# A hybrid attention and mixture-of-experts layer on one core: the weight units' place in memory, and the place of a conditional part

## The chip, the core and the metric

The kernel runs on one core of a Trainium2 chip. The time is the device time of one execution in microseconds (us), the median of several runs. One core has a matrix engine (TensorE, PE in the profile; PEld is its weight load), a vector engine (VectorE, DVE), a scalar engine (ScalarE, ACT), GpSimd (POOL), and SyncE (SP), which here only issues transfers. 16 DMA engines move data between the chip's main memory (HBM) and the core's on-chip memory (SBUF: 128 partitions). TensorE writes to PSUM, eight banks of 128 x 512 float32.

## The reference

One layer over 256 latent tokens of 1024 features, with 256 context tokens. The front half is a modulated layer norm, one input projection, neighbourhood attention beside a spatial gating unit, an output projection and a layer norm. The back half, where the change is, is a mixture of 32 experts with four chosen for each token:

```python
def moe_ffn(h, router_w, router_b, w_gu, b_gu, w_down, b_down):
    logits = t @ router_w + router_b
    top_vals, top_idx = lax.top_k(logits, TOP_K)          # 4 of 32
    gates = jax.nn.softmax(top_vals, axis=-1)
    ...
    def expert_step(acc, xs):
        gu = t @ wgu + bgu                                # 1024 x 2048
        gate = jnp.minimum(gu[:, :D_FF_EXPERT], SWIGLU_LIMIT)
        lin = jnp.clip(gu[:, D_FF_EXPERT:], -SWIGLU_LIMIT, SWIGLU_LIMIT)
        y = ((lin + 1) * (gate * jax.nn.sigmoid(SWIGLU_ALPHA * gate))) @ wd + bd   # 1024 x 1024
        return acc + wgt[:, None] * y, None
...
x = layer_norm(DEEPNORM_ALPHA * x + g2 * ffn_x, ln2_g, ln2_b)
```

All is float32. An expert's weights are 12 MB, those of all experts 384 MB (in units of 2^20 bytes), and each is read once.

## The kernel before

**Groups and slots.** Experts are ranked on the chip by how many tokens chose them, and worked off in 13 groups: group 0 holds experts 0 and 1, then come groups of one, two or four ranks in the order of `PLAN` (L35). A group always makes one matmul of 128 token slots: one rank has 128 slots, each of a pair 64, each of four 32. The last group, number 12, has four ranks. For every group the tokens are gathered by a one-hot matmul (`gather`), go through four gate-up steps (`gu_step`, L1105, each over 512 columns, with `swiglu_gate` or `swiglu_lin` behind it), are transposed (`h_T`), go through the down projection in two halves of 512 columns (`down`, L1152), are scaled by the gate vector (`scaled`, L1184) and are added to the accumulator `acc` by a one-hot matmul (`scatter`, L1165). The scatter of a group is put off into the next one (`pending`, run at its hook "gu1"). The last group does its own: it scatters the first half between the two halves of `down`, and its second half is added in two PSUM banks, `sums`, that an identity matmul of `acc` has started (`last_sums`, L1178, at the hook "in2", in the middle of the group's gate-up part).

**The conditional part.** Tokens beyond a rank's slots are taken by `overflow_items` (L1238): every engine loads the number of items, and under `tc.If(n_items > 0)` (L1240) a loop runs one more group of 128 slots for each item, weights and all. With the inputs of this case the number is zero and the body is skipped. The part stands ahead of group 5 (the second group of one rank). Ahead of it, group 4's scatter is run at once, and from group 4 on four weight units are kept free for the loop's own loads (`reserve[0] = 4`, L1318).

**Weights.** SBUF holds 26 units (`NU`, L38) of 128 x 2048 float32, 8 KB in each partition, in the pool `uni`. A unit is taken for a weight piece or for other data. Pieces stand in one list, `stream`, in the order of use; `pump` (L138) takes a free unit and has SyncE issue the load, and `done` (L151) releases a unit behind its last matmul and pumps the next piece. One expert is eight gate-up pieces and four down pieces of 1 MB; in the last group the second half's later pieces are cut smaller (`DOWN_ROWS`, L37). SyncE works its list in order: an issue waits until the unit's last reader is done. In the last group, six units hold other data.

**Order.** The order of instructions on each engine is that of the program text (`manual_schedule`). The pools are placed in SBUF in the order of their making: the constants, `cst`, come first, then `uni`. Constants are rounded up to 32 bytes.

Of the kernel before, what the change touches and what calls it, by code (L numbers as in the profile page):

```python
# [9 lines left out]
F32 = mybir.dt.float32  # L10
# [8 lines left out]
P = 128  # L19
# [3 lines left out]
TT = NTOK // P  # L23
# [14 lines left out]
NU = 26  # L38
# [27 lines left out]
def hybrid_layer_kernel(  # L66
# [12 lines left out]
    router_w = router_w[0]  # L79
    w_gu, b_gu, w_dn, b_dn = exp_w_gu, exp_b_gu[0], exp_w_down, exp_b_down[0]  # L80

    cst = ctx.enter_context(tc.tile_pool(name="cst", bufs=1))
    uni = ctx.enter_context(tc.tile_pool(name="uni", bufs=1))
    mo = ctx.enter_context(tc.tile_pool(name="mo", bufs=2))
    sm = ctx.enter_context(tc.tile_pool(name="sm", bufs=4))
    pm = ctx.enter_context(tc.tile_pool(name="pm", bufs=4, space=bass.MemoryType.PSUM))
# [5 lines left out]
    def nm(s):  # L92
        uid[0] += 1
        return f"{s}_{uid[0]}"

    def mm_bank():
        return pm.tile([P, 512], F32, tag="mm", name=nm("mm"))
# [40 lines left out]
    def pump(n=1, keep=0):  # L138
        while n > 0 and stream and len(free_slots) > keep:
            key, fn = stream.pop(0)  # L140
            t = unit("w")
            loaded[key] = (t, fn(t))
            n -= 1
# [12 lines left out]
    reserve = [0]  # L156
# [2 lines left out]
        return bass.AP(tensor=src.tensor, offset=src.offset, ap=[[0, parts], [1, n]])  # L159


    ident = cst.tile([P, P], F32, name="ident")
    make_identity(nc, ident)
    mhalf = cst.tile([P, 1], F32, name="mhalf")
    G.memset(mhalf, -0.5)


# [551 lines left out]
    late, zst = {}, {}  # L719
# [445 lines left out]
    def scatter(ys, st, nns=range(2)):  # L1165
        for nn in nns:
            t2_free(ys[nn])
            for t in range(TT):
                b = ax_bank()
                PE.matmul(b, st[:, t, :], ys[nn], start=True, stop=True)  # L1170
                sl = acc[t][:, nn * 512:(nn + 1) * 512]
                V.tensor_tensor(sl, sl, b, op=ALU.add)  # L1172
                if zst2:
                    ln_half(zst2[t], acc[t], nn)
# [3 lines left out]
    def last_sums():  # L1178

        for t in range(TT):  # L1180
            sums.append(ax_bank())
            PE.matmul(sums[t], ident, acc[t][:, 512:D], start=True, stop=False)

    def scaled(bank, nn):  # L1184
        y = t2("y")
        t2_hold(y)
        V.tensor_tensor(y, bank, late_v["g2"][:, nn * 512:(nn + 1) * 512], op=ALU.mult)  # L1187
        return y

    def group(n, gid, cur, sel, hooks):  # L1190
        xg = cur[0]

        def hook(name):
            for f in hooks.get(name, ()):
                f()

        b = gu_step(n, gid, 0, 0, xg, sel, lambda: hook("in0"))
        if gid == 0:
            hook("gu0")
        g_0 = swiglu_gate(b)  # L1200
        if gid != 0:
            hook("gu0")
        b = gu_step(n, gid, 1, 0, xg, sel, lambda: hook("in1"))
        l_0 = swiglu_lin(b, g_0)
        hook("gu1")
        b = gu_step(n, gid, 0, 1, xg, sel, lambda: hook("in2"))
        g_1 = swiglu_gate(b)
        h0 = h_T(l_0)
        hook("gu2")
        b = gu_step(n, gid, 1, 1, xg, sel, lambda: hook("in3"))  # L1210
        l_1 = swiglu_lin(b, g_1)
        yb = [mm_bank() for _ in range(2)]
        if gid == len(groups) - 1:
            hs = (h0, h_T(l_1))
            zst2.extend(sm.tile([P, 2, 6], F32, tag="zst", bufs=2, name=nm("zst")) for _ in range(TT))
            down(n, gid, hs, 0, yb[0], last=True)
            ys = [scaled(yb[0], 0)]
            scatter(ys, cur[1], [0])
            down(n, gid, hs, 1, yb[1], last=True)
            y = scaled(yb[1], 1)  # L1220
            for t in range(TT):
                PE.matmul(sums[t], cur[1][:, t, :], y, start=False, stop=True)
                V.bn_stats(zst2[t][:, 1, :], sums[t])
            return None
        hs = [h0]
        down(n, gid, hs, 0, yb[0], 0, 4)
        hs.append(h_T(l_1))
        down(n, gid, hs, 0, yb[0], 4)
        ys = [scaled(yb[0], 0)]
        down(n, gid, hs, 1, yb[1])  # L1230
        for h in hs:
            t2_free(h)
        ys.append(scaled(yb[1], 1))
        return lambda: scatter(ys, cur[1])
# [3 lines left out]
    def overflow_items():  # L1238
        n_items = nc.values_load(nit[0:1, 0:1], min_val=0, max_val=NE)
        with tc.If(n_items > 0):  # L1240
            with tc.For_i(0, n_items) as it:
                ps_ = mo.tile([P, 2, TT, 1], F32, tag="ipos", bufs=1, name="ipos")
                for a in range(2):
                    V.tensor_copy(ps_[:, a], late_v["itm"][:, a, :, ds(it, 1)])
                sc_ = mo.tile([P, 1], F32, tag="isel", bufs=1, name="isel")
                V.tensor_copy(sc_, prs_[:, ds(it, 1)])
                ie = mo.tile([1, 1], I32, tag="iexp", bufs=1, name="iexp")
                V.tensor_copy(ie, iei[0:1, ds(it, 1)])
                rest = stream[:]
                stream.clear()  # L1250
                group_stream("x", [(ie, 0)])
                oh = make_oh(ps_[:, 0], 1, P)
                sel = make_sel(sc_)
                xg = gather(oh)
                st = weigh_T(weigh(oh, ps_[:, 1]))
                group(1, "x", (xg, st), sel, {})()
                stream.extend(rest)
# [5 lines left out]
    for gi, rk in enumerate(groups):  # L1263
        n = 2 if rk is None else len(rk)
        nxt = groups[gi + 1] if gi + 1 < len(groups) else None
        box = {}
        hooks = {k: [] for k in ("in0", "gu0", "in1", "gu1", "in2", "gu2", "in3")}

        def prep():
            a, m = nxt[0], len(nxt)  # L1270
            box["oh"] = make_oh(late_v["pcr"][:, 0, :, a:a + m], m, P // m)
            box["sel"] = make_sel(perm[:, a:a + m])
            box["ohg"] = weigh(box["oh"], late_v["pcr"][:, 1, :, a:a + m])

        def fetch():
            box["cur"] = [gather(box["oh"]), None]
            box["cur"][1] = weigh_T(box["ohg"])

        def streams():
            for g2_, rk2 in enumerate(groups[1:], 1):  # L1280
                group_stream(g2_, [(ordi, rr) for rr in rk2], g2_ == len(groups) - 1)
            pump(NU)

        def first_T():
            cur[1] = weigh_T(ohg0)

        if gi == 0:
            hooks["in0"] += [rank_counts]
            hooks["gu0"] += [rank_order, streams]
            hooks["gu1"] += [finish_G]  # L1290
            hooks["in1"] += [lambda: by_rank(late_v["pcr"], perm[0:NE, :])]
            hooks["gu1"] += [first_T, prep]
        else:
            if nxt:
                hooks["gu0"] += [prep]
            hooks["gu1"] += [pending]
        if gi == 1:
            hooks["in0"] += [lambda: acc_init((0, 1))]
            hooks["gu0"] += [lambda: acc_init((2, 3))]
            reserve[0] = 2  # L1300
        if gi == 2:
            ovf_u, l2_u = unit("ovf"), unit("l2")
            reserve[0] = 0
            for k, f in zip(("in0", "in1", "in2", "in3"), overflow_steps(ovf_u[:, 0:512])):
                hooks[k] += [f]
            S.dma_start(l2_u[0:1, 0:D], ln2_g)
            S.dma_start(l2_u[0:1, D:2 * D], ln2_b)
        if nxt:
            hooks["gu2"] += [fetch]
        if gi == 4:  # L1310
            def spread(js):
                for j in js:
                    b = ax_bank()
                    PE.matmul(b, ident[0:1, 0:1].to_broadcast([1, P]), l2_u[0:1, j * 512:(j + 1) * 512], start=True, stop=True)
                    S.copy(l2_u[:, j * 512:(j + 1) * 512], b)
            hooks["in1"] += [lambda: spread((0, 1))]
            hooks["in2"] += [lambda: spread((2, 3))]
            reserve[0] = 4  # L1318
        if gi == 5:
            pending()  # L1320
            hooks["gu1"].remove(pending)
            overflow_items()

            xg_i[0] ^= 1
            mo.tile([P, TT, P], F32, tag="sT", name=nm("sT"))
            mo.tile([P, 1, P], F32, tag="sel", name=nm("sel"))
            reserve[0] = 0
            pump(NU)
        if gi == len(groups) - 1:
            hooks["in2"] += [last_sums]  # L1330
        pending = group(n, gi, cur, sel_now, hooks)
        if gi == 2:
            release(ovf_u)
            pump(1)
        if nxt:
            cur, sel_now = box["cur"], box["sel"]
# [80 lines left out]
```

## Time and profile before

| what | us |
|---|---|
| median of 3 runs | 1139.0 (1137.99 to 1139.81) |
| the profiled execution, its own time | 1136.04 |
| its span, first to last instruction | 1134.3 |
| TensorE matmuls busy | 997.4 (88%) |
| VectorE busy | 306.0 (27%) |
| ScalarE busy | 132.8 (12%) |

The transfers are 451 MB (10^6 bytes), a mean of 398 GB/s over the span. In the profile a line such as L1160 is that of the source; a group of instructions is written as output <- inputs by the program's names, with the count and the busy time, and in brackets the idle time just before it and what ended it. `w` is a weight unit, `mm` and `ax` are PSUM banks, `t` a scratch tile. A float32 matmul appears as two matmul records. "PEclk" is the TensorE clock that was granted, as a share of the full one. A DMA share of 1.00 means that all 16 engines are busy, and it can come out slightly over that.

### The profile page before, as it was taken

Reading aid. Unit: us, or ns where it says so; the run is one execution under the profiler, and the core shown is the slowest. Engines: PE = TensorE matmul, PEld = TensorE weight load, DVE = VectorE, ACT = ScalarE, POOL = GpSimd, SP = SyncE. Lnnn points to the kernel's source line nnn. Section 1 sums busy time; section 2 is a strip of 40 time slices with the busy share of each in tenths; the row PEclk is TensorE's granted clock in tenths of the full one; section 3 lists DMA queues with packets and bytes.
Section 4 is the critical chain, followed back from the end, with each engine's and each line's share of the span. In section 5 each row is a group of like instructions: output and inputs, shape, how many; then the busy total and the mean of one; then the engine's idle time right before and its main releaser. Section 6 shows DMA issues by size and latency. Waiting matters only on the chain. (4 is left out here: it accounts for less than half of the span.)

```text
span 1134.3 us, 13253 instructions
## 1 busy us (share of the span) xinstructions
PE 997.4 (88%) x5140; PEld 421.6 (37%) x5140; DVE 306.0 (27%) x621; ACT 132.8 (12%) x286; POOL 27.7 (2%) x57
## 2 busy tenths in 40 slices
PE   5999897999779999986799999987799999977765
PEld 4897465333214433321253434222134343421111
DVE  6596765314103121210121212111021211201003
ACT  4343342100100101110010101000001010100000
POOL 2000300000000000000000000000000000000000
PEclk9999898999989999988999999988899999999988
DMA  9998599799999999999989999999999999999995
GB/s 381 421 396 325 229 360 366 307 386 422 420 421 421 421 420 421 422 420 421 420 343 422 421 421 420 421 422 421 421 422 420 420 422 420 421 422 421 421 420 190
DMA packets 66296, 451.32 MB, mean 398 GB/s; under 512 B 8627, under 2 KB 8883, under 8 KB 12725
## 3 DMA queue, kind: packets, MB, share of 16 engines
q1 hardware_dynamic: 66082, 450.03, 96.4%
q8 instruction: 42, 0.69, 0.2%
q10 hardware_dynamic: 148, 0.40, 0.1%
q14 instruction: 24, 0.20, 0.0%
HBM read 449.36 MB, written 1.05 MB: 397 GB/s over the span
## 5 line engine op out<-in xcount | busy, mean ns | idle before, releaser
L1114 PE MATMUL mm<-w,xg 128*32 128x512 f32 (+2 forms) x2048 | 424.9, 620 | 42.7 <-DMA w<-in_exp_w_gu_dram 42.7
L1160 PE MATMUL mm<-w,t 128*32 128x512 f32 (+2 forms) x1024 | 235.2, 645 | 52.2 <-DMA w<-in_exp_w_down_dram 43.6
L1114 PEld LDWEIGHTS mm<-w,xg 128*32 128x32 f32 (+2 forms) x2048 | 127.9, 130 | 325.6 <-issue 242.4
L1160 PEld LDWEIGHTS mm<-w,t 128*32 128x32 f32 (+2 forms) x1024 | 67.4, 133 | 207.9 <-issue 109.9
L1187 DVE TENSOR_TENSOR t<-mm,late 128x512 f32<-128x512 f32 x26 | 18.0, 692 | 263.0 <-PE mm L1160 263.0
L1130 ACT ACTIVATE t<-t 128x512 f32<-128x512 f32 x26 | 16.4, 630 | 583.0 <-DVE t L1128 583.0
L1137 DVE TENSOR_SCALAR t<-mm 128x512 f32<-128x512 f32 x26 | 18.0, 692 | 222.7 <-PE mm L1114 222.7
L1128 DVE TENSOR_SCALAR t<-mm 128x512 f32<-128x512 f32 x26 | 18.0, 691 | 215.4 <-PE mm L1114 215.4
L894 PE MATMUL mm<-bgu,sel 32*128 32x512 f32 x104 | 58.4, 641 | 4.0 <-PEq L1240 4.0
L1170 PE MATMUL ax<-t,sT 128*128 128x512 f32 x100 | 46.3, 605 | 0.8 <-DVE t L1187 0.8
L888 PE MATMUL ax<-oh,tM 128*128 128x128 f32 x384 | 44.8, 275 | 0.0
L888 PEld LDWEIGHTS ax<-oh,tM 128*128 128x128 f32 x384 | 43.8, 192 | 0.0
L1149 ACT COPY t<-ax 128x512 f32<-128x512 f32 x26 | 15.0, 576 | 190.6 <-PE ax L1145 190.6
L245 POOL TENSOR_TENSOR rs<-rs,mhalf 128x1 f32<-128x1 f32 x12 | 9.5, 797 | 1047.4 <-DVE mv L257 919.5
L1172 DVE TENSOR_TENSOR xin<-xin,ax 128x512 f32<-128x512 f32 x50 | 33.2, 684 | 5.2 <-PE ax L1170 4.8
L1170 PEld LDWEIGHTS ax<-t,sT 128*128 128x128 f32 x100 | 18.0, 189 | 29.2 <-issue 24.6
L894 PEld LDWEIGHTS mm<-bgu,sel 32*128 32x128 f32 x104 | 15.3, 183 | 34.3 <-issue 24.5
L780 ACT ACTIVATE xg<-ax,sh,sc 128x128 f32<-128x128 f32 x60 | 22.4, 457 | 32.3 <-PE ax L888 26.5
L414 DVE TENSOR_TENSOR wlo<-w,whi 128x1024 fp32r<-128x1024 f32 x20 | 23.7, 1223 | 3.1 <-ACT whi L411 3.1
L411 ACT CAST whi<-w 128x1024 fp32r<-128x1024 f32 x20 | 20.1, 1047 | 9.5 <-PE mm L446 9.5
L1145 PEld LDWEIGHTS ax<-ident,t 128*128 128x128 f32 x104 | 11.2, 141 | 21.8 <-issue 16.8
L525 DVE SCALAR_TENSOR_TENSOR accB<-w,front,accB 128x2048 f32<-128x2048 f32 x8 | 18.8, 2348 | 0.0
(261 smaller groups left out, 717.8 us busy)
## 6 DMA issues: line engine op xcount, KB each, us to landing
w<-in_exp_w_gu_dram SPq DMA_DIRECT2D x256, 1024.0 KB, 19.8
w<-in_exp_w_down_dram SPq DMA_DIRECT2D x124, 1024.0 KB, 19.8
w<-in_w_front_dram SPq DMA_DIRECT2D x38, 1024.0 KB, 10.7
w<-in_exp_w_down_dram SPq DMA_DIRECT2D x4, 512.0 KB, 16.1
w<-in_exp_w_down_dram SPq DMA_DIRECT2D x8, 256.0 KB, 6.9
T<-in_rpb_dram SPq DMA_DIRECT2D x2, 768.0 KB
xin<-in_x_dram SPq DMA_DIRECT2D x2, 512.0 KB
cin<-in_ctx_dram SPq DMA_DIRECT2D x2, 512.0 KB, 6.4
```

The source lines that it names most:

```text
L411: S.copy(av[:, k], w[:, k])
L414: V.tensor_tensor(bv[:, k], w[:, k], av[:, k].bitcast(F32), op=ALU.subtract)
L525: V.scalar_tensor_tensor(accB_u, w[:, 0, :], sT[:, k, 0:1], accB_u, op0=ALU.mult, op1=ALU.add)
L780: S.activation(dst[:, kk, :], src, AF.Identity, scale=sc2[:, kk:kk + 1], bias=sh2[:, kk:kk + 1])
L888: PE.matmul(bank[:, k * P:(k + 1) * P], late["tMv"][:, t, (hh * 4 + k) * P:(hh * 4 + k + 1) * P], oh[:, t].rearrange("p n w -> p (n w)"), ...
L894: PE.matmul(b, sel[r, :], bgu[r, :], start=True, stop=False)
L1114: PE.matmul(b[a * w:(a + 1) * w, :], xg[:, half * 4 + k, a * w:(a + 1) * w], weights((gid, part, j, half, a))[:, k, :], start=False, stop= ...
L1128: V.tensor_scalar_min(gtile, b, 7.0)
L1137: V.tensor_scalar(lt, b, 7.0, -7.0, op0=ALU.min, op1=ALU.max)
L1160: PE.matmul(bank[a * w:(a + 1) * w, :], hs[kk // 4][:, kk % 4 * P + a * w:kk % 4 * P + (a + 1) * w], weights((gid, nn, r0, a))[:, k, :], s ...
L1170: PE.matmul(b, st[:, t, :], ys[nn], start=True, stop=True)
L1172: V.tensor_tensor(sl, sl, b, op=ALU.add)
```

## The change

First, the pool `uni` is made ahead of `cst`, behind a new pool `pad` of 128 bytes that holds the small constant `mhalf`; so all weight units lie at other addresses. Second, the conditional part moves from ahead of group 5 into the last group, behind the first half of the down projection and its scaling. With it go the early scatter of group 4, the four reserved units and the two tiles taken only to keep a rotation in step. As the loop body uses the same PSUM banks, the last group takes its second output bank, the `sums` banks with their identity matmuls, and the tiles of the last statistics behind the conditional part; `last_sums` leaves the hook "in2".

```diff
@@ -79,8 +79,10 @@
     router_w = router_w[0]
     w_gu, b_gu, w_dn, b_dn = exp_w_gu, exp_b_gu[0], exp_w_down, exp_b_down[0]
 
+
+    pad = ctx.enter_context(tc.tile_pool(name="pad", bufs=1))
+    uni = ctx.enter_context(tc.tile_pool(name="uni", bufs=1))
     cst = ctx.enter_context(tc.tile_pool(name="cst", bufs=1))
-    uni = ctx.enter_context(tc.tile_pool(name="uni", bufs=1))
     mo = ctx.enter_context(tc.tile_pool(name="mo", bufs=2))
     sm = ctx.enter_context(tc.tile_pool(name="sm", bufs=4))
     pm = ctx.enter_context(tc.tile_pool(name="pm", bufs=4, space=bass.MemoryType.PSUM))
@@ -159,9 +161,9 @@
         return bass.AP(tensor=src.tensor, offset=src.offset, ap=[[0, parts], [1, n]])
 
 
+    mhalf = pad.tile([P, 32], F32, name="mhalf")[:, 0:1]
     ident = cst.tile([P, P], F32, name="ident")
     make_identity(nc, ident)
-    mhalf = cst.tile([P, 1], F32, name="mhalf")
     G.memset(mhalf, -0.5)
 
 
@@ -1209,12 +1211,16 @@
         hook("gu2")
         b = gu_step(n, gid, 1, 1, xg, sel, lambda: hook("in3"))
         l_1 = swiglu_lin(b, g_1)
-        yb = [mm_bank() for _ in range(2)]
+        last = gid == len(groups) - 1
+        yb = [mm_bank() for _ in range(1 if last else 2)]
         if gid == len(groups) - 1:
             hs = (h0, h_T(l_1))
-            zst2.extend(sm.tile([P, 2, 6], F32, tag="zst", bufs=2, name=nm("zst")) for _ in range(TT))
             down(n, gid, hs, 0, yb[0], last=True)
             ys = [scaled(yb[0], 0)]
+            overflow_items()
+            yb.append(mm_bank())
+            last_sums()
+            zst2.extend(sm.tile([P, 2, 6], F32, tag="zst", bufs=2, name=nm("zst")) for _ in range(TT))
             scatter(ys, cur[1], [0])
             down(n, gid, hs, 1, yb[1], last=True)
             y = scaled(yb[1], 1)
@@ -1315,19 +1321,6 @@
                     S.copy(l2_u[:, j * 512:(j + 1) * 512], b)
             hooks["in1"] += [lambda: spread((0, 1))]
             hooks["in2"] += [lambda: spread((2, 3))]
-            reserve[0] = 4
-        if gi == 5:
-            pending()
-            hooks["gu1"].remove(pending)
-            overflow_items()
-
-            xg_i[0] ^= 1
-            mo.tile([P, TT, P], F32, tag="sT", name=nm("sT"))
-            mo.tile([P, 1, P], F32, tag="sel", name=nm("sel"))
-            reserve[0] = 0
-            pump(NU)
-        if gi == len(groups) - 1:
-            hooks["in2"] += [last_sums]
         pending = group(n, gi, cur, sel_now, hooks)
         if gi == 2:
             release(ovf_u)
```

## Rows read from the trace of the kernel before

**Rows 1.** The page's DMA engine shares over the whole span: 40 slices of 28.4 us, tenths

```profile
DMA  9998599799999999999989999999999999999995
```

**Rows 2.** Windows: length; busy (count) PE, PEld, DVE, ACT, POOL; PEclk, DMA share, GB/s

```profile
240.00:580.00 340.00, 300.81 (x1444) 107.50 (x1441) 63.25 (x135) 19.89 (x42) 0.00 (x0) 0.96 1.01 421
...
580.00:590.00 10.00, 10.00 (x52) 6.46 (x51) 2.66 (x6) 2.87 (x7) 0.00 (x0) 1.00 0.56 200
...
590.00:1105.00 515.00, 455.09 (x2088) 157.04 (x2086) 81.67 (x154) 27.40 (x59) 0.00 (x0) 0.97 1.01 421
```

**Rows 3.** Loads of tile w issued by SyncE from 590 to 1060 us

```profile
DMA to landing us min/median/max: 16.5/19.8/20.7
```

**Rows 4.** Instructions of line 1240, the branch, on each sequencer: ns min/median/max, starts

```profile
L1240 SPq EVENT_SEMAPHORE  x9: 17/17/17, 566.6 to 585.7; - x9
...
L1240 PEldq COMPARE_BRANCH  x1: 6127/6127/6127, 550.1 to 550.1; - x1
...
L1240 DVEq COMPARE_BRANCH  x1: 72/72/72, 553.1 to 553.1; - x1
...
L1240 SPq COMPARE_BRANCH  x1: 53/53/53, 566.1 to 566.1; - x1
```

**Rows 5.** TensorE's timeline around that branch: start, us, engine, line [idle before]

```profile
548.69 3.70 PE L1170 MATMUL ax<-t,sT 128*128 128x512 f32 x8
...
556.44 1.41 PE L894 MATMUL mm<-bgu,sel 32*128 32x512 f32 x2 [4.04 <-PEq L1240]
...
557.78 4.60 PE L1114 MATMUL mm<-w,xg 128*128 128x512 f32 x7
```

**Rows 6.** DMA engines' shares from 579 to 590 us: 40 slices of 0.275 us, tenths

```profile
DMA  9997997666653334300130000000890049999999
```

**Rows 7.** Timeline of the last group's down projection, engines as named

```profile
1095.05 0.14 PEld L1160 LDWEIGHTS mm<-w,t 128*32 128x32 f32 x2 [2.25 <-DMA w<-in_exp_w_down_dram]
...
1097.54 0.14 PEld L1160 LDWEIGHTS mm<-w,t 128*32 128x32 f32 x2 [2.35 <-DMA w<-in_exp_w_down_dram]
...
1100.01 5.20 PE L1160 MATMUL mm<-w,t 128*32 128x512 f32 x26 [1.43 <-DMA w<-in_exp_w_down_dram]
...
1105.99 1.98 PE L1170 MATMUL ax<-t,sT 128*128 128x512 f32 x4 [0.78 <-DVE t L1187]
...
1109.98 3.63 PE L1160 MATMUL mm<-w,t 128*32 128x512 f32 x30 [1.02 <-DMA w<-in_exp_w_down_dram]
...
1110.43 0.13 PEld L1160 LDWEIGHTS mm<-w,t 128*32 128x32 f32 x4 [0.30 <-issue]
...
1110.86 0.13 PEld L1160 LDWEIGHTS mm<-w,t 128*32 128x32 f32 x4 [0.30 <-issue]
...
1113.79 0.14 PEld L1160 LDWEIGHTS mm<-w,t 128*32 128x32 f32 x2 [1.08 <-DMA w<-in_exp_w_down_dram]
...
1115.04 0.16 PEld L1160 LDWEIGHTS mm<-w,t 128*32 128x32 f32 x8 [1.11 <-DMA w<-in_exp_w_down_dram]
...
1116.33 0.14 PEld L1160 LDWEIGHTS mm<-w,t 128*32 128x32 f32 x2 [0.30 <-DMA w<-in_exp_w_down_dram]
...
1120.22 0.14 PEld L1160 LDWEIGHTS mm<-w,t 128*32 128x32 f32 x2 [0.50 <-DMA w<-in_exp_w_down_dram]
...
1121.30 0.69 DVE L1187 TENSOR_TENSOR t<-mm,late 128x512 f32<-128x512 f32 x1 [11.42 <-PE mm L1160]
```

**Rows 8.** SyncE's own issues in the last group and at the end, same timeline

```profile
1062.12 53.32 SPq L225 DMA_DIRECT2D w<-in_exp_w_down_dram  x24
...
1126.91 4.75 SPq L1348 DMA_DIRECT2D out_dram<-xin  x4
```

**Rows 9.** The two identity matmuls of the final sums, in TensorE's timeline

```profile
1053.16 1.98 PE L1182 MATMUL ax<-xin,ident 128*128 128x512 f32 x4
```

**Rows 10.** Two windows after a pause of TensorE, columns as in rows 2

```profile
1100.00:1104.00 4.00, 3.99 (x24) 1.03 (x25) 0.00 (x0) 0.00 (x0) 0.00 (x0) 0.60 1.02 424
...
556.40:560.40 4.00, 3.96 (x5) 1.47 (x6) 0.00 (x0) 0.00 (x0) 0.00 (x0) 0.59 1.03 424
```

## The prediction

> **What bounds the kernel now.** I read the page's slices first: the DMA engines are at nine tenths or more from the ninth slice (227 us) to the last but one, except for the twenty-first [rows 1]. The windows say it in numbers: 421 GB/s at a DMA share of 1.01 from 240 to 580 us, the same from 590 to 1105 us, and 200 GB/s in the ten between [rows 2]. So from about 232 us the kernel is a stream of expert weights, and its end is the landing of the last weight plus a fixed tail. Is anything else able to stop the stream? SyncE keeps eight loads under way: issue to landing is 19.8 us in the median, and in 590 to 1060 us never under 16.5 us [rows 3], against 2.49 us that one MB takes (the starts at 1095.05 and 1097.54 us, each released by a landing [rows 7]). TensorE thus never lets the queue run dry. The one hole is at 581 to 588 us.
>
> **Why the hole is there.** The conditional part (L1240) isn't taken: none of its matmuls run. What it leaves on SyncE is one branch at 566.1 us and nine semaphore events from 566.6 to 585.7 us [rows 4]. I read these as the skipped path paying the semaphore counts of the eight load lanes, each after its last load has landed: SyncE issues nothing meanwhile, the eight loads under way drain, and the stream starts from empty. TensorE pays at another time: its branch takes 6.1 us [rows 4], of which 4.04 us show as idle, from the last scatter matmul's end at 552.4 to 556.44 us [rows 5]. VectorE's branch takes 0.07 us [rows 4].
>
> **Part 1: the conditional part leaves group 5.** TensorE's 4.04 us there are worth nothing by themselves, as the stream sets the pace. The hole is. By bytes it is (421 - 200)/421 x 10 = 5.25 us of the 16 DMA engines' mean [rows 2]. But the engines don't stop together: the share falls in steps from 581 us and is zero in seven slices of 0.275 us, 1.9 us, only [rows 6]. I read a load's landing as the end of its last part. If the engine that was last at the hole is also the last at the end, it wins 1.9 us; if the lag was evenly shared, 5.25 us. No row tells which. I take the middle, 3.6 us, and keep 1.9 and 5.25 as ends. The reserve of four units and the early scatter go too; the scatter's eight matmuls, 3.70 us [rows 5], move to the usual place beside the next group's work, and cost the same there. Nothing else becomes late, since the landing times of [rows 3] leave 16.5 us of cover, and TensorE starts group 5 earlier by 4.04 us as well.
>
> **Part 2: it enters the last group.** On SyncE it costs nothing. The weight units left after six held for other data are 20; with 32 gate-up units done and four of the first down half, 20 + 32 + 4 = 56 loads, all of the last group's, stand ahead of the branch. SyncE issues the last of them at 1115.4 us [rows 8], its semaphore events then end with the last landing, about 1120.3 us, and the first output transfer is issued at 1126.9 us [rows 8]. TensorE stands behind its own branch, and behind TensorE wait the scatter of the first half, the two identity matmuls that start the final sums (L1182, moved here from the middle of the group), and the second down half. In times of before: the first half's matmuls end at 1105.21 us [rows 7]; VectorE's scaling (L1187, 0.69 us) [rows 7] and its short branch lie beside the stall. With 4.04 us as in [rows 5] TensorE goes on at 1109.25 us. Then come the sums' matmuls, 1.98 us [rows 9], the scatter, 1.98 us, and the second half: four column-packed matmuls each 0.43 us (weight loads at 1110.43 and 1110.86 us [rows 7]), so 64 in 6.9 us. The sum is 1120.1 us. The last weight lands at 1120.22 us and VectorE takes the result at 1121.30 us [rows 7]: TensorE just catches up, cost 0. But after the stall at 552 us the granted clock was 0.59 over the next 4 us [rows 10], that is 3.3 us at 1.2 GHz and the rest at 2.4; at a granted clock of 0.60, 26 matmuls took 5.20 us at 1100 us, while 30 took 3.63 us at 1110 us [rows 7, 10]. That adds some 1.65 us: 1121.8 against 1121.3 us, 0.5 us late; if the second half can't be packed as tightly as that between landings (30 matmuls in 3.63 us [rows 7] make 64 in 7.7 us), 1.4 us late. I take 0.6 us, ends 0 and 1.4.
>
> **Part 3: the units' place.** By the tile sizes in the code, the first unit now begins at byte 9888 of a partition (160 past a multiple of 256), behind the constants; with the constants moved behind it and a 128-byte pad ahead, at byte 512. All units shift alike. No engine instruction changes its shape, and each start is a multiple of 32 bytes before and after. What could move is the per-row cost of a transfer. Its bound: two 512 KB pieces (1113.79 to 1115.04 us, 1.25 us each) take 0.01 us more than one of 1 MB at 2.49 us; four of 256 KB (0.648 us each, seven starts 1116.33 to 1120.22 us) 0.10 us more [rows 7]. What doesn't grow with the bytes is thus 0.01 to 0.035 us of a 1 MB load, and alignment can save at most that: over 888 us / 2.49 us = 357 loads, 3.6 to 12.5 us. The lower end of a gain is 0, and so is my value, as the nearer piece in size leaves hardly anything. A loss I exclude but for noise, as the same bytes go the same way.
>
> Here the Trainium skill speaks the other way, in "DMA: Bandwidth & Descriptors", "How a descriptor splits into AXI transactions": a piece that doesn't begin on 256 bytes pays for the unused bytes ahead of its start too. An 8 KB row from 160 would cost 261 beats of 32 bytes, not 256; by that estimate 1.9% of 888 us, 17 us, go away. It is more than the whole fixed cost that the trace leaves, but it is the direction of the first rival.
>
> And of the branch, "Advanced Engine Details and Errata", "Control Flow Timing", says about 108 ns for a compare and branch; VectorE's row agrees, TensorE's 6.1 us doesn't, and by the page's figure the tail would cost nothing.
>
> **The sum.** -3.6 + 0.6 + 0 = -3.0 us. The profiled execution has a span of 1134.3 us and took 1136.04 us, 1.7 us around it; it lies 3.0 us under the median of the runs shown, 1139.0 us. The profiled one would become 1133.0 us, and the median **1136.0 us**, 0.26% less. A measurement of this kernel can tell about 0.2%, 2.3 us, from no change.
>
> **The rivals.**
> A, the forecast: the gain at the hole less the tail, -1.9 + 1.4 = -0.5 to -5.25 us, so 1133.8 to 1138.5 us. For it: the hole is the only one, and its cause is a line that leaves. Chance 0.66, three quarters of it beyond 2.3 us.
> B, alignment counts: a transfer's fixed cost falls by the 3.6 to 12.5 us above, beside A: 1123.5 to 1132.4 us, middle 1128. For it: the 1 MB loads are the whole kernel. Against it: the fixed cost must almost vanish. Chance 0.12.
> C, the gain is eaten (or the change doesn't do what it says): the engine that is last stays the last, and TensorE resumes late; or a load still stands behind the branch on SyncE, and the drain comes back with a hole of 2 to 5 us before the last pieces. 1137 to 1140 us. Against the latter: the count of 56. Chance 0.14.
> D, slower: TensorE's first matmul behind the branch waits for what SyncE pays only after the last landing. Then the sums, the scatter and the second half, 1.98 + 1.98 + 6.9 = 10.9 us, begin at about 1120.5 us and end at 1131.4 us, 10.1 us late; with 3.6 us gained, 1145.5 us. It decides from a stall of 8.9 us on (1105.2 + 8.9 + 10.9 = 1121.3 + 3.7), against 4.04 us. Against it: at 557.78 us TensorE used weights loaded ahead of the branch, 8 us before SyncE came to its own [rows 4, 5]. Chance 0.08.
>
> **How the numbers follow.** The likeliest case gives 1136.0 us. The range, 1129.0 to 1139.3 us, holds A, nearly all of C and the smaller gains of B; left out are D and the larger half of B with C's rim, some 0.2. Faster by over 0.2%: three quarters of A and all of B, 0.50 + 0.12 = 0.62. Within 0.2%: a quarter of A, and C, 0.30. Slower: D, 0.08.
>
> **What would show it.** Right: 421 GB/s without a gap from 240 to 1100 us; no idle on TensorE near 552 us; TensorE idle some 4 us after the first down half of the last group, its branch near 6 us; the last scaling within 1.5 us behind the last landing plus 1.1 us. Step by step wrong: the last landing earlier by under 1.9 or over 5.3 us (part 1); TensorE still at work on the second half well after the last landing (part 2); 1 MB loads landing faster than 2.49 us apart, or a steady rate off 421 GB/s (part 3). The forecast falls if TensorE waits at its branch for SyncE, or if the rate changes.

## The result, and the profile after

The changed kernel takes 1122.58 us (median; 1121.35 to 1124.87) against 1138.49 us, a ratio of 0.9866 [0.984, 0.9893]: 15.3 us less by the ratio, 15.9 us by the medians. The forecast was 3.0 us less, with 1129.0 us as the low end of the range. The profiled execution of the changed kernel took 1124.87 us with a span of 1123.1 us, 11.2 us under that of before.

The page of the changed kernel, its DMA engine shares and GB/s in 40 slices of 28.1 us:

```profile
DMA  9997779699999999999999999999999999999994
GB/s 376 425 380 294 291 293 399 268 386 426 427 427 426 427 426 427 426 427 427 426 427 426 427 426 427 427 427 426 426 427 427 426 427 427 427 426 427 427 425 163
```

Against [rows 1] the dent in the twenty-first slice is gone. The rate is the news: 426 or 427 GB/s in every slice from the tenth to the thirty-eighth, where [rows 2] had 421. The windows of the changed kernel, the last of 4 us from the end of TensorE's stall (below), columns as in rows 2 (length; busy and count of PE, PEld, DVE, ACT, POOL; granted clock, DMA share, GB/s):

```profile
240.00:560.00 320.00, 284.80 (x1428) 101.33 (x1425) 60.24 (x131) 19.89 (x42) 0.00 (x0) 0.97 1.01 426
580.00:590.00 10.00, 10.00 (x31) 4.77 (x30) 1.21 (x4) 1.76 (x5) 0.00 (x0) 1.00 1.02 429
590.00:1085.00 495.00, 438.34 (x2043) 152.55 (x2041) 80.84 (x153) 27.40 (x59) 0.00 (x0) 0.97 1.01 427
...
1094.60:1098.60 4.00, 3.99 (x12) 1.57 (x16) 1.11 (x2) 0.00 (x0) 0.00 (x0) 1.00 0.90 357
```

The second row answers to the hole of 200 GB/s in [rows 2]: 429. The first and third show the engines as full as before (share 1.01), but moving 1.2 and 1.4% more. Over the 880 us from 240 us to the last landing, (1 - 421/427) x 880 = 12.4 us, to within some 1.5 us, as the rates are rounded to 1 GB/s.

The branch of the conditional part, now line 1246, on each sequencer (ns min/median/max, starts):

```profile
L1246 SPq EVENT_SEMAPHORE  x9: 17/17/17, 1104.0 to 1109.4; - x9
...
L1246 PEldq COMPARE_BRANCH  x1: 5849/5849/5849, 1088.4 to 1088.4; - x1
...
L1246 DVEq COMPARE_BRANCH  x1: 72/72/72, 1092.0 to 1092.0; - x1
...
L1246 SPq COMPARE_BRANCH  x1: 53/53/53, 1103.5 to 1103.5; - x1
```

These answer to [rows 4]: the same branch of about 6 us on TensorE and the same nine events on SyncE, now behind the last issue. The timeline of the changed kernel's last down projection (start, us, engine, line, [idle before]):

```profile
1087.67 3.62 PE L1162 MATMUL mm<-w,t 128*32 128x512 f32 x26 [1.41 <-DMA w<-in_exp_w_down_dram]
...
1094.61 1.96 PE L1184 MATMUL ax<-xin,ident 128*128 128x512 f32 x4 [3.31 <-PEq L1246]
...
1096.40 1.88 PE L1172 MATMUL ax<-t,sT 128*128 128x512 f32 x4
...
1098.21 10.44 PE L1162 MATMUL mm<-w,t 128*32 128x512 f32 x62
...
1103.77 0.14 PEld L1162 LDWEIGHTS mm<-w,t 128*32 128x32 f32 x2 [0.27 <-DMA w<-in_exp_w_down_dram]
...
1105.71 0.14 PEld L1162 LDWEIGHTS mm<-w,t 128*32 128x32 f32 x2 [0.52 <-DMA w<-in_exp_w_down_dram]
...
1109.01 0.14 PEld L1162 LDWEIGHTS mm<-w,t 128*32 128x32 f32 x2 [1.27 <-SPq L1246]
...
1110.10 0.69 DVE L1189 TENSOR_TENSOR t<-mm,late 128x512 f32<-128x512 f32 x1 [9.91 <-PE mm L1162]
...
1115.71 4.75 SPq L1341 DMA_DIRECT2D out_dram<-xin  x4
```

TensorE idles 3.31 us behind its branch, does the sums and the scatter, and has worked off what lies ready of the second half when the last piece lands: the last weight load starts at 1109.01 us, against 1120.22 us in [rows 7], and VectorE's scaling follows 1.09 us later, against 1.08 us. So the end is still the last landing plus a fixed tail, and it came 11.2 us earlier. The view names an event of SyncE's branch as what released the last weight load. It stands for the landing: in the trace's semaphore records that load's last part lands at 1108.97 us, SyncE's event follows at 1108.99 and TensorE's weight load at 1109.01 us.

Why 11.2 us here and 15.3 us over all runs? Two stretches of this execution take some of the gain back. One is the front part, ahead of the stream. The first 240 us, before, then after:

```profile
0.00:240.00 240.00, 215.40 (x1489) 146.50 (x1491) 146.81 (x306) 82.66 (x178) 26.52 (x55) 0.97 0.87 348
```

```profile
0.00:240.00 240.00, 214.50 (x1473) 147.49 (x1475) 145.50 (x304) 82.73 (x178) 26.52 (x55) 0.96 0.86 342
```

In these two executions the changed kernel has 6 x 0.24 = 1.4 MB less loaded by then, 3.4 us of the stream. Of the kernels below, the two that differ least from this one, e4 and e8, show 342 GB/s there too, the place alone 346 and the move alone 347. So it is more than one execution's accident; its cause stays open, and the intervals of the times below are too wide to tell such a term. The other stretch is the end. The last seven weight loads of 256 KB pieces start from 1103.77 to 1109.01 us, 5.24 us, where [rows 7] had 3.89 us (1116.33 to 1120.22): 1.35 us more. The hole's 3.8 us (measured below) and the rate's 12.4, less 3.4 and 1.35, make 11.4 us.

### The profile page after: what moved, and what is told of

Same layout as the page of the kernel before. It is cut to its first block, busy times and chain, and to the rows that moved or that the text cites. A ratio compares the mean times of both kernels' runs of the same rounds, so it can differ in the third digit from the quotient of the medians.

```text
span 1123.1 us, 13259 instructions
## 1 busy us (share of the span) xinstructions
PE 989.3 (88%) x5140; PEld 422.3 (38%) x5140; DVE 305.9 (27%) x621; ACT 132.9 (12%) x286; POOL 27.7 (2%) x57
## 5 line engine op out<-in xcount | busy, mean ns | idle before, releaser
L1116 PE MATMUL mm<-w,xg 128*32 128x512 f32 (+2 forms) x2048 | 416.9, 615 | 38.6 <-DMA w<-in_exp_w_gu_dram 38.6
L1116 PEld LDWEIGHTS mm<-w,xg 128*32 128x32 f32 (+2 forms) x2048 | 127.3, 129 | 314.0 <-issue 233.6
L896 PEld LDWEIGHTS mm<-bgu,sel 32*128 32x128 f32 x104 | 15.3, 183 | 30.9 <-issue 20.7
L1147 PEld LDWEIGHTS ax<-ident,t 128*128 128x128 f32 x104 | 11.2, 140 | 21.8 <-issue 16.8
## 6 DMA issues: line engine op xcount, KB each, us to landing
w<-in_exp_w_down_dram SPq DMA_DIRECT2D x4, 512.0 KB, 15.9
```

Of the source, the lines that this page charges most:

```text
L896: PE.matmul(b, sel[r, :], bgu[r, :], start=True, stop=False)
L1116: PE.matmul(b[a * w:(a + 1) * w, :], xg[:, half * 4 + k, a * w:(a + 1) * w], weights((gid, part, j, half, a))[:, k, :], start=False, stop= ...
```

## The experiments

Two theories for the unforeseen part: **the place of the units** raised the rate (the prediction's rival B), or **the moved conditional part** is worth more than its hole. Each part of the change was run alone.

**The place alone, e1_align_only.** The kernel before with the pools in the new order; the conditional part stays ahead of group 5.

```diff
-    cst = ctx.enter_context(tc.tile_pool(name="cst", bufs=1))
+    pad = ctx.enter_context(tc.tile_pool(name="pad", bufs=1))
     uni = ctx.enter_context(tc.tile_pool(name="uni", bufs=1))
+    cst = ctx.enter_context(tc.tile_pool(name="cst", bufs=1))
...
+    mhalf = pad.tile([P, 32], F32, name="mhalf")[:, 0:1]
-    mhalf = cst.tile([P, 1], F32, name="mhalf")
```

> The kernel before with the units at byte 512 and nothing else; the conditional part stays ahead of group 5. Theory S (the place of the units sped up the stream, the move only removed the hole): 357 loads of 1 MB from 232 us on, each 0.035 us shorter (2.49 to 2.455 us, as the landings of the changed kernel stand apart), so 12.5 us less: 1126 us, ratio 0.989; steady rate 427 GB/s on both sides of the hole, and the hole is still there. Rival H (the hole was worth more than I priced, and the two parts feed each other, the stream being faster because it is never drained): 3 to 8 us less, ratio 0.993 to 0.997, rate near 421 GB/s.

Measured: 1125.22 us against 1137.84, ratio 0.9888 [0.9864, 0.9911], 12.6 us less by the medians. Its windows:

```profile
240.00:560.00 320.00, 281.41 (x1404) 99.60 (x1401) 59.55 (x126) 19.26 (x41) 0.00 (x0) 0.95 1.01 426
580.00:590.00 10.00, 10.00 (x52) 6.47 (x51) 2.66 (x6) 2.87 (x7) 0.00 (x0) 1.00 0.72 285
590.00:1080.00 490.00, 437.75 (x2043) 155.14 (x2045) 81.66 (x154) 27.40 (x59) 0.00 (x0) 0.97 1.01 427
```

The hole is still there (285 GB/s in its ten us) and the rate on both sides is that of the changed kernel. The place makes the rate. The single packets in the traces, one for each partition's row of a load, show it directly: from 590 to 1050 us one of 8 KB took 314.1 ns in the mean before, and 309.4 ns both here and in the changed kernel.

**The move alone, e2_move_only.** The changed kernel with the pools in their old order, units at byte 9888.

```diff
-    pad = ctx.enter_context(tc.tile_pool(name="pad", bufs=1))
-    uni = ctx.enter_context(tc.tile_pool(name="uni", bufs=1))
     cst = ctx.enter_context(tc.tile_pool(name="cst", bufs=1))
+    uni = ctx.enter_context(tc.tile_pool(name="uni", bufs=1))
...
-    mhalf = pad.tile([P, 32], F32, name="mhalf")[:, 0:1]
+    mhalf = cst.tile([P, 1], F32, name="mhalf")
```

> The changed kernel with the units back behind the constants at byte 9888; the conditional part is in the last group. Theory S: steady rate 421 GB/s, no hole, 3.0 us less than before (0.5 to 5.25): 1135.5 us, ratio 0.9974. Rival H: rate 427 GB/s, ratio 0.987 to 0.990.

Measured: 1134.58 us, ratio 0.9977 [0.9964, 0.999], 2.6 us less by the ratio, 3.3 us by the medians. Its windows around the old hole, and then a line of TensorE's timeline with a window of the 3 us from there:

```profile
580.00:590.00 10.00, 10.00 (x43) 5.72 (x42) 2.06 (x5) 2.30 (x7) 0.00 (x0) 1.00 1.02 423
590.00:1080.00 490.00, 436.70 (x1993) 150.65 (x1995) 80.26 (x152) 26.88 (x58) 0.00 (x0) 0.96 1.01 421
```

```profile
1104.47 3.14 PE L1183 MATMUL ax<-xin,ident 128*128 128x512 f32 x4 [3.08 <-PEq L1245]
```

```profile
1104.50:1107.50 3.00, 3.00 (x5) 1.21 (x6) 0.00 (x0) 0.00 (x0) 0.00 (x0) 0.60 0.79 307
```

No hole, and the old rate; TensorE stalls 3.08 us at the branch and is granted 0.60 of its clock behind it, mostly the lower of its two levels (1.2 and 2.4 GHz). Both ways of counting add up: 12.6 + 3.3 = 15.9 us by the medians, 12.7 + 2.6 = 15.3 us by the ratios. The three intervals leave some 4 us either way; what shows that neither part needs the other is the windows, the old rate without the hole here and the new rate with it there.

**The two ends of the move, e3_before_no_cond and e4_after_no_cond.** What the conditional part costs at either place: the kernel before without it, and the changed kernel without it.

```diff
-            reserve[0] = 4
-        if gi == 5:
-            pending()
-            hooks["gu1"].remove(pending)
-            overflow_items()
...
-            reserve[0] = 0
-            pump(NU)
```

```diff
             ys = [scaled(yb[0], 0)]
-            overflow_items()
             yb.append(mm_bank())
```

> The kernel before without the conditional part, which is not taken with these inputs, and without the four reserved units and the early scatter; the loop is left out. It prices the hole alone: S says 3.6 us less, ends 1.9 (the slowest DMA engine's idle time) and 5.25 (the mean engine's): 1134.9 us, ratio 0.9954 to 0.9983, and 0.6 us less than the move alone. H: more than 6 us.

> The changed kernel without the conditional part; the loop is left out and all else stays in its order. It prices TensorE's stall in the last group: S says it is hidden, 0 to 1.4 us less than the changed kernel, 0.6 taken; 1122 us, ratio to before 0.986. A rival (the stall delays the second down half to the end): 3 to 4 us less, ratio 0.983.

Measured: without it the kernel before takes 1134.04 us, ratio 0.9967 [0.9953, 0.9981], 3.8 us less; the hole, at 421 GB/s now, is worth that:

```profile
580.00:590.00 10.00, 10.00 (x37) 5.25 (x36) 1.35 (x4) 1.76 (x5) 0.00 (x0) 1.00 1.01 421
```

The changed kernel without it takes 1123.05 us, 0.986 [0.9835, 0.9885] against 0.9866 with it: some 0.7 us (0.0006 of 1138), with a half width (half the 95% interval of the difference) of some 4 us, so the runs don't tell it from nothing. In its timeline TensorE's stall is gone, and the last seven weight loads start over 3.86 us, not 5.24:

```profile
1091.03 1.98 PE L1184 MATMUL ax<-xin,ident 128*128 128x512 f32 x4
...
1103.57 0.14 PEld L1162 LDWEIGHTS mm<-w,t 128*32 128x32 f32 x2 [0.29 <-DMA w<-in_exp_w_down_dram]
...
1107.43 0.14 PEld L1162 LDWEIGHTS mm<-w,t 128*32 128x32 f32 x2 [0.49 <-DMA w<-in_exp_w_down_dram]
```

**Which places are good, e5 to e8.** The changed kernel with other pads: the first unit at byte 416 (a multiple of 32), 448 (of 64), 384 (of 128, the pad left out: 384 bytes are taken ahead of all pools), and 9984 (of 256 and not of 512, constants ahead of the units as in the kernel before). The diffs are those of 416 (448 has 16 in place of 8) and of 9984. If the order of the pools did it, the first three would be fast and the last slow.

```diff
-    mhalf = pad.tile([P, 32], F32, name="mhalf")[:, 0:1]
+    mhalf = pad.tile([P, 8], F32, name="mhalf")[:, 0:1]
```

```diff
+    cst = ctx.enter_context(tc.tile_pool(name="cst", bufs=1))
     pad = ctx.enter_context(tc.tile_pool(name="pad", bufs=1))
     uni = ctx.enter_context(tc.tile_pool(name="uni", bufs=1))
-    cst = ctx.enter_context(tc.tile_pool(name="cst", bufs=1))
```

> The changed kernel with a pad of 32 bytes, so the units, still ahead of the constants, begin at byte 416 (32 past a multiple of 64). Theory P (the address counts, not the order of the pools): 421 GB/s and 2.49 us for a 1 MB load, 1135 us, ratio 0.9977 as with the move alone. Rival O (the order of the pools, or where the constants lie, counts): 427 GB/s, 1122.6 us, ratio 0.9866.

> The same with a pad of 64 bytes: units at byte 448, a multiple of 64 but 64 past one of 128 and 192 past one of 256. If a multiple of 64 is enough: 427 GB/s, 1122.6 us, ratio 0.9866. If a row must begin on 256 bytes: 421 GB/s or a little over, 1132 to 1135 us. In between if the cost goes by how far the row begins into a block.

> The same with no pad: units at byte 384, a multiple of 128 but 128 past one of 256. If a multiple of 64 or 128 is enough: 427 GB/s, 1122.6 us. If a row must begin on 256 bytes: about 421 GB/s, 1132 to 1135 us.

> The changed kernel with the constants ahead of the units, as before, and a pad between them, so that the units begin at byte 9984: a multiple of 256, 256 past one of 512. Theory P: 427 GB/s, 1122.6 us, ratio 0.9866, the order of the pools is nothing. Rival O: 421 GB/s, 1135 us. If a multiple of 512 were needed: about 421 GB/s too.

| first unit at byte | us | ratio [95%] | GB/s, 590 to 1080 us |
|---|---|---|---|
| 416 = 256 + 160 | 1134.95 | 0.9982 [0.9966, 0.9997] | 421 |
| 448 = 256 + 192 | 1135.73 | 0.9983 [0.9969, 0.9996] | 421 |
| 384 = 256 + 128 | 1134.35 | 0.9975 [0.9958, 0.9992] | 421 |
| 9984 = 39 x 256 | 1125.17 | 0.989 [0.9858, 0.9923] | 427 |

The windows of 384, then of 9984:

```profile
590.00:1080.00 490.00, 436.63 (x1996) 150.94 (x1998) 80.27 (x152) 26.86 (x58) 0.00 (x0) 0.96 1.01 421
```

```profile
590.00:1080.00 490.00, 433.53 (x2030) 153.06 (x2032) 80.28 (x152) 27.44 (x59) 0.00 (x0) 0.98 1.01 427
```

Of the starts tried, those on 256 bytes are fast and no others; 512 gives nothing more that can be told, 128 gives nothing, and the order of the pools is not it. The three bad places stand where the move alone stood. The packets of 8 KB took 314.2, 314.2 and 314.0 ns at 416, 448 and 384, and 309.4 ns at 9984.

**Is it TensorE reading the units? e9_few_matmuls_9888 and e10_few_matmuls_512.** The weights are also what TensorE loads, so its reads could have become cheaper, or got out of the way of the writes. The kernel before and the changed kernel, each with only the first and last of every eight gate-up and down matmuls.

```diff
+                wk = weights((gid, part, j, half, a))
+                if half * 4 + k in (0, 7):
-                PE.matmul(b[a * w:(a + 1) * w, :], xg[:, half * 4 + k, a * w:(a + 1) * w],
+                    PE.matmul(b[a * w:(a + 1) * w, :], xg[:, half * 4 + k, a * w:(a + 1) * w],
...
+                    if kk in (0, 7):
```

> The kernel before with only the first and the last of every eight matmuls of the gate-up and down steps; the other six are left out, all loads stay. TensorE reads a quarter of the weights. Theory D (the loads hinder one another or themselves when a row begins off a boundary): the steady rate stays at 421 GB/s, away from the hole. Rival T (TensorE's reads of the same memory hinder the loads): it rises to 424 to 427 GB/s. The time falls by at most a few us either way, as the stream sets it.

> The changed kernel with the same six of eight matmuls left out: units at byte 512. Both theories: 427 GB/s; it is the other side of the comparison. Beside the run at byte 9888, D says 10 to 14 us between the two, T under 5 us, with some 3 us of either from the moved part.

Measured: 1133.62 us, 0.996 [0.9945, 0.9975], and 1120.7 us, 0.9823 [0.976, 0.9886]. The windows of the first, then of the second:

```profile
590.00:1080.00 490.00, 362.32 (x759) 90.95 (x758) 77.13 (x143) 25.64 (x56) 0.00 (x0) 0.75 1.01 422
```

```profile
590.00:1080.00 490.00, 351.90 (x765) 85.96 (x764) 75.91 (x142) 26.18 (x57) 0.00 (x0) 0.79 1.01 427
```

With matmuls and weight loads down from some 2000 to 760, the rates are 422 and 427, and 12.9 us lie between the two, some 3 of it the move's. The second kernel has two runs only, so its time is known to some 7 us; the packets settle it, with 314.0 and 309.2 ns. What TensorE reads has no part in it. The granted clock, 0.75 and 0.79 in the mean of its two levels now that TensorE idles longer between its matmuls, costs the stream nothing either.

**Once per row, or with the bytes? e11_short_rows_9888 and e12_short_rows_512.** In a load every partition's 8 KB is one row of the transfer. Two kernels write each weight unit in rows of 2 KB, the same bytes (some 196,000 packets of 2 KB in the trace, in place of some 49,000 of 8 KB), at the old and at the new place (the second is the place alone with this edit); the blocks are stored in reverse, so that the transfer can't be joined into one row, and the matmuls read them so.

```diff
-                SP.dma_start(t, expert(src, a)[i])
+                SP.dma_start(t.rearrange("p (k n) -> p k n", n=512)[:, ::-1, :],
+                             expert(src, a)[i].rearrange("p (k n) -> p k n", n=512))
...
-                          weights((gid, part, j, half, a))[:, k, :], start=False, stop=half == 1 and k == 3)
+                          weights((gid, part, j, half, a))[:, 3 - k, :], start=False, stop=half == 1 and k == 3)
```

> The kernel before with the expert weights loaded in rows of 2 KB: each 1 MB load puts its four blocks of 512 columns in reversed order, and the matmuls read them so; units at byte 9888. More and shorter rows cost by themselves: the 256 KB pieces, which have such rows, stood 0.645 us apart in the changed kernel, 2.58 us per MB against 2.45, so some 46 us more. Beside the run at byte 512, theory X (the cost of a bad start is paid once in each row) says four times the 12.6 us of 8 KB rows, 40 to 50 us between the two: 1210 to 1225 us here. Theory Y (it goes with the bytes) says 12 to 14 us again: 1180 to 1190 us.

> The same reversed blocks in the kernel whose units begin at byte 512 and whose conditional part is still ahead of group 5. Both theories: some 46 us more than the same kernel with 8 KB rows, about 1171 us and 405 GB/s; it is the other side of the comparison.

Measured: 1217.14 us, 1.0706 [1.0668, 1.0744], and 1165.86 us, 1.0248 [1.023, 1.0267]. The windows of the first, then of the second:

```profile
600.00:1050.00 450.00, 400.36 (x1731) 144.45 (x1732) 77.16 (x153) 27.99 (x62) 0.00 (x0) 0.96 1.04 382
```

```profile
600.00:1050.00 450.00, 407.90 (x1839) 147.17 (x1841) 76.20 (x148) 27.95 (x62) 0.00 (x0) 0.97 1.04 404
```

51.3 us lie between the two places, 4.07 times the 12.6 us of the long rows, with four times the rows: the cost of a bad start is paid once per row. With 357 loads of 128 rows over 16 DMA engines (eight rows on each, taking the rows as spread evenly), 12.6 us / (357 x 8) = 4.4 ns a row, and 51.3 us / (357 x 32) = 4.5 ns. The packets say the same: 314.1 against 309.4 ns for 8 KB, 88.7 against 84.2 ns for 2 KB, 4.7 and 4.5 ns. What happens in a DMA engine in these 4.5 ns no run here shows.

## Why the prediction was right or wrong

**What bounds the kernel: right.** The stream sets the time from some 232 us on. TensorE's matmuls cut by more than half moved the time by under 6 us, and a rate up by 1.4% moved it by 1.1%.

**Part 1, the hole: right, its size by luck.** 3.6 us forecast, 3.8 measured by taking the conditional part away, with 2.2 to 5.3 us as the interval. The ends, 1.9 and 5.25 us, held it, and without the part the hole is gone. But the value was the middle of two ends that no row decided between, and the interval covers nearly all of what lies between them. The lower end was also read short: the share in [rows 6] is 0 in eleven slices, 3.0 us, seven of them in a row. The reserve of four units and the early scatter were taken away with the part in every run; that the draining queue is the cause, and not these, the trace of the kernel before shows. SyncE issues no load from 565.1 to 586.0 us. Its last eight events each wait for the semaphore of one load lane: six of them stand 0.01 or 0.02 us behind a landing on it, from 573.15 to 585.53 us, the loads of the last two had landed before, and the next issue starts at 585.97 us.

**Part 2, the tail: right in order, its size not shown.** 0.6 us forecast; by the runs 0.7 us with a half width of some 4 us (with and without the part in the last group), or 1.1 us with one of some 2 us (the move alone against the kernel before without the part). The order came out as counted: SyncE's events run from 1104.0 to 1109.4 us, behind its last issue, and TensorE did 62 matmul records of the second half from 1098.21 us on, before they ended, so rivals C (a load behind the branch) and D (TensorE waits for what SyncE pays) fall.

What the forecast of the tail didn't have is that the last landings come slower: 5.24 us over the last seven starts, and 4.13 to 4.63 us in four others with the part there (e5 to e8), against 3.86 and 3.89 us in the two that leave the part out. The place alone, with the part ahead of group 5, shows 4.65 us, so it need not be the part's doing; the cause stays open. The half clock that the forecast took over from [rows 10] came in the move alone (0.60, the identity matmuls 3.14 us) and not in the changed kernel (1.00, 2.4 GHz throughout, 1.96 us): after a pause of 3.08 us at the one and 3.31 us at the other. Three more kernels with the part there (e5, e6, e8) paused for 2.08, 3.53 and 2.62 us and did the identity matmuls in 1.95 or 1.96 us, so the length of the pause alone doesn't decide. Which of them the other executions met isn't known. The prediction's word that VectorE's row "agrees" is too kind: 0.07 us is two thirds of the figure quoted there.

**Part 3, the place: wrong, and it is the whole miss.** The term was set to 0, with 12.5 us as the far end; 12.6 was measured. The mechanism stood in the text as rival B, with 0.12, at 1123.5 us at its far end and 1128 in the middle; the measured 1122.58 us lies just beyond that far end. The step that failed is the choice of the low end of the bound, "as the nearer piece in size leaves hardly anything"; the value of 0 stood even under that end, 3.6 us. It took the 512 KB pieces' excess of 0.01 us per MB in [rows 7] for the measure of what a row costs. Halving the piece doubles the rows per MB, so the idea was sound, but the row was too coarse: the short rows show 79.4 us / (357 x 24) = 9.3 ns for each further row at the old place, so 8 further rows per engine should have cost 0.074 us per MB, and the 24 of the 256 KB pieces 0.22 us, where [rows 7] gave 0.01 and 0.10 us. The changed kernel shows that these pieces don't carry the term: at the good place they still start 0.647 us apart (1103.77 to 1105.71 us), against 0.648, where eight rows of 4.5 ns ask for 0.036 us less. A few pieces at the end of the stream, read from the starts of their readers to 0.01 us, can't stand for a term that counts 357 times.

The upper end was no measurement either. The fixed cost per row at the old place is 0.074 us per load, taking each row to cost what a further one does, twice the 0.035 us taken as its most; the part that goes away with the start on 256 bytes, 12.6 us / 357 = 0.035 us, agrees with that bound by chance. "Against it: the fixed cost must almost vanish" was thus wrong too: half of it vanished. At the new place (1165.86 - 1125.22) us / (357 x 24) = 4.7 ns per row are left.

What spoke for B was a rule, and it was right in direction. The Trainium skill, "DMA: Bandwidth & Descriptors", "How a descriptor splits into AXI transactions", has a piece pay for the unused bytes ahead of a start off 256 bytes. It tells it of reads; what moved here is the start of the written side. The runs agree on the 256 and on a cost once per row. They don't agree on the size: its estimate was 17 us, against 12.6. Nor do they show the grading by the unused bytes: 128, 160 and 192 of them gave 1134.35, 1134.95 and 1135.73 us. Scaled to the measured 12.6 us for 160 bytes, the rule asks for 5 us between the first and the last; the ratios differ by 0.0008, with a half width of some 0.0022, so 0.9 +- 2.5 us. The packets tell it more closely: 314.0, 314.2 and 314.2 ns, where the rule, scaled to the 4.8 ns of 160 bytes, asks for 1.9 ns between the first and the last.

**The chances.** The range left out the larger half of B, although nothing in the trace excluded it: its far end was this kernel's own rows, multiplied out. With the term's two ends an open question, the honest range reached to 1123.5 us, and to 1121.3 us with the hole at its far end too (1139.0 - 12.5 - 5.25).

## What to carry to other kernels

Where a stream of transfers sets the time, look at where its rows begin in SBUF: with rows of 8 KB a start off 256 bytes cost 1.1% of this kernel, with rows of 2 KB 4.2%. A cost that counts once per row or per load of the bounding stream is a large term at any size that the trace can't exclude: keep its far end in the range, or measure it over hundreds of loads and not over the last few. The conditional part, skipped as it was, made the issuing queue wait for its loads under way, 3.8 us here; behind the last issue no such hole is left.

## What was unexpected of the hardware

The DMA share reads 1.01 at 421 and at 427 GB/s alike, and 1.04 at 382 and 404: the time lost on a bad start or on short rows counts as busy, so a full share is no proof of a full rate. What shows the loss is the mean time of a packet of one size.

TensorE's jump over the skipped part took 5.85 us in the changed kernel, 3.31 of it seen as idle, with 6.13 and 4.04 us at the old place [rows 4, 5]; VectorE's took 0.07 us at both. In the other kernels with the part TensorE's took 5.08 to 6.32 us, but 0.37 and 0.35 us in the two with few matmuls, whose skipped body holds fewer matmuls too; that it goes by the length of that body is a guess that no run tests alone. The granted clock after it was 0.59 in [rows 10], 0.60 in the move alone and 1.00 in the changed kernel.
